# Seven block products for both FFN output products of a diffusion layer, with weight sums made by accumulating DMAs

## The chip, the cores and the metric

One core of a Trainium2 chip runs the whole layer as one program. The metric is the device time of one execution in microseconds (us). TensorE (PE in the profile) multiplies, VectorE (DVE) and ScalarE (ACT) work on tiles in SBUF and PSUM, GpSimd (POOL) adds tiles and can issue DMAs, and SyncE (SP) issues DMAs. Each engine carries out its own instructions in order, and waits at an instruction until what it reads and overwrites is ready.

## The reference

The layer works on 1024 latent tokens and 256 context tokens of width 1024. It has a half-step FFN, a token mixer and a second half-step FFN, and ends with an RMSNorm. The part that is changed:

```python
def swiglu(h, w_in, w_out):
    a, b = jnp.split(h @ w_in, 2, axis=-1)
    return (jax.nn.silu(a) * b) @ w_out
...
x = x + 0.5 * ml[2] * swiglu(modulate(rms_norm(x, norm1_g[layer]), ml[0], ml[1]),
                              ffn1_w_in[layer], ffn1_w_out[layer])
...
x = x + 0.5 * ml[8] * swiglu(modulate(rms_norm(x, norm3_g[layer]), ml[6], ml[7]),
                              ffn2_w_in[layer], ffn2_w_out[layer])
return rms_norm(x, final_g)
```

The hidden width D_FF is 2816, which is 22 row blocks of 128. Everything is float32.

## The kernel before

Activations lie transposed in SBUF: 128 channels on the partitions, tokens along the row. The latent tokens are two chunks of 512, C0 and C1. A float32 product is made of three products in the faster float32r format: each operand is split into a high part (a cast, on ScalarE) and a low part (the source less the high part, a subtraction on VectorE; `split`, L186), and high·high, high·low and low·high are summed in PSUM. So one 128x128 block of weights against 512 tokens costs three matmuls.

The FFN's in-product (class `Winograd`, L463 to 740) already uses a scheme with seven products instead of eight. It makes the hidden rows j = 0 to 21, both chunks of one j at a time. Its right operands, the tiles r of eight kinds (28 tiles for one FFN), stay in SBUF meanwhile.

The **out-product of FFN1** (L1029 to 1066) is a plain product. The hidden rows were stored in DRAM (`hd`, by `spill`, L963) and are loaded again, 256 KB each, and split; for each chunk and each group of three output blocks d the columns of w_out are loaded (`load_w`, L202), split and multiplied: 8 d x 22 j x 2 chunks x 3 = 1056 matmuls of 512 columns. At the end of each group the result is scaled by a gate and added to x (a SCALAR_TENSOR_TENSOR on VectorE). Between them, in C0, the generator `steps` is run four steps at a time; it makes the adaLN modulation from w_mod (`later_mod`, L261: loads of 256 KB called rawm, and accumulations macc on VectorE). In C1 the generator `norms2` (`norm0`, L499) is run, which prepares chunk C0 for the mixer: sum of squares, rstd, scaling, and the split into r1 and r2.

The **out-product of FFN2** (`ffn`, L742 to 786) is woven into its in-product: after every two hidden rows j come their 96 matmuls into all eight blocks d and both chunks, and each result is added to x at once, 16 adds for each of 11 pairs. The hidden rows never leave SBUF. In the last pair C1 is done as two halves of 256 columns, so that the final norm of C0 (`final`, L1488) runs beside them.

Between both FFNs lies the mixer: the mix stage (L1070 to 1112) makes gates and convolution inputs, attention follows.

The tile pools set what can run ahead: the A pool has 38 slots of 4 KB a partition (x, r, hidden rows and much else; `A_BUFS`), raw weights have 3 buffers, split weights wl and wh 4 each, short-lived tiles (`ttile`) 11; PSUM has five banks under the tag s (names ps), two under t (pt) and one under o (po). A scheduler orders the instructions of each engine by data and buffers; SyncE's queue holds nearly all DMAs. Because every instruction is recorded in one helper, the profile gives L88 for all; the tile names tell them apart.

Of the kernel before, what the change touches and what calls it, by code (L numbers as in the profile page):

```python
# [49 lines left out]
def tile_dit_layer(  # L50
# [79 lines left out]
    def matmul(out, w, x, start, stop, pinned=False):  # L130
        inst = pe.matmul(out, w, x, start=start, stop=stop)
        if pinned:
            tc.keep_in_program_order(inst)
# [329 lines left out]
    class Winograd:  # L463
# [6 lines left out]
        def __init__(self, xs, gain, mod, m, pairs, plain=False, ahead=3, side_from=None):  # L470
# [9 lines left out]
            self.n_ahead, self.side, self.started, self.n_left = ahead, None, [], 0  # L480
            self.source, self.ready = self.lefts(pairs, side_from), []
# [32 lines left out]
        def square(self, d):  # L514

            if d == 0:
                self.acc = [ttile("sq_acc")]
            sq = self.acc[0] if d == 0 else ttile("sq")
            act.activation(out=sq, in_=self.xs(d, C1), func=AF.Square)
            if d == KD - 1:  # L520
                self.acc.append(sq)
            elif d:
                dve.tensor_add(out=self.acc[0], in0=self.acc[0], in1=sq)

# [217 lines left out]
        def ffn(self, w_o, gate, last_chunks, after):  # L742
            def hidden(a, b, j, ch):

                if j % 2 == 0:
                    t = atile("hid", (P, 2, 512), F32R)
                    g = t[:, 0], t[:, 1]
                else:
                    g = ttile("gh", dt=F32R), ttile("gl", dt=F32R)
                act.activation(out=a, in_=a, func=AF.Silu)  # L750
                dve.tensor_mul(out=a, in0=a, in1=b)
                split(a, *g)
                hid[j, ch] = g

            for pr in range(NH // 2):
                hid = {}
                js = (2 * pr, 2 * pr + 1)
                if pr == 0:
                    self.start(self.norm1())
                for j in js:  # L760
                    u, c = self.next_first()
                    v, b = self.second(u)
                    hidden(c, b, j, C0)
                    hidden(*self.third(u, v), j, C1)
                ws = out_pieces(w_o, js)
                if pr < NH // 2 - 1:
                    self.prefetch(3)
                for ch in (C0, C1) if pr < NH // 2 - 1 else last_chunks:
                    s, o, n = ch
                    full = (C0, C1)[o // 512]  # L770
# [340 lines left out]
    for k in range(4):  # L1111
        mix.part_second(k)
# [462 lines left out]
```

## Time and profile before

| quantity | value |
|---|---|
| time, median of 3 runs | 2805.99 us (2802.83 to 2806.69) |
| profiled execution, time | 2801.0 us |
| profiled execution, span of its trace | 2799.2 us |
| granted TensorE clock, mean | 0.987 |
| matmuls | 13741 |
| DMA, mean | 108 GB/s |

The span is divided into busy time by engine; the chain is the sequence of instructions and waits that ended last. A window row gives, for one stretch of time, the busy time and number of instructions of each engine, then the granted clock of TensorE, the share of the DMA engines and their GB/s. A row of groups reads: engine, operation, output <- inputs (without the numbers of buffers), shapes and count, then busy time in us and mean ns of one, then the idle time just before and what ended it. A timeline row gives the start and length in us, and in brackets the idle time before it.

### The profile page before, as it was taken

To read this page: it belongs to the slowest core of one execution; us is meant where nothing else is said; L and a number is where in the kernel's file an instruction comes from. 1 tells how busy PE (TensorE), PEld (TensorE's weight loads), DVE (VectorE), ACT (ScalarE), POOL (GpSimd) and SP (SyncE) were. 2 spreads that over 40 slices of the span, in tenths; PEclk is the share of its full clock that TensorE was granted. 3 is DMA by queue.
4 is the path that set the end of the run, shared out by engine and by line. 5 is a ranking of instruction groups with operands and counts; after the bars stand their busy time and mean duration, and the time that the engine had idled before them with its cause. 6 is when DMAs were issued, how large, how long until landed. Compare 5 with 4: busy or idle time off the path is not lost.

```text
span 2799.2 us, 36980 instructions
## 1 busy us (share of the span) xinstructions
PE 2716.4 (97%) x13741; PEld 2280.3 (81%) x13741; DVE 1956.4 (70%) x3269; ACT 1105.1 (39%) x2177; POOL 502.6 (18%) x383
## 2 busy tenths in 40 slices
PE   7898999999999989999999999999998999999998
PEld 4687988888888867888999888877886788888887
DVE  5887688877854398676478676675458766666667
ACT  4524333333433243333244665674235222332225
POOL 2240122121000043323023111000002221212110
PEclk8899999999999999999999999999999999999999
DMA  8264434445974333322312321002433311111111
GB/s 305 95 204 156 143 107 128 131 145 162 314 237 126 103 123 106 98 90 77 119 33 84 95 80 46 27 31 80 158 91 103 101 46 46 61 61 53 46 53 68
DMA packets 355229, 302.96 MB, mean 108 GB/s; under 512 B 25558, under 2 KB 284776, under 8 KB 355048
## 3 DMA queue, kind: packets, MB, share of 16 engines
q1 hardware_dynamic: 355048, 300.59, 33.3%
q8 instruction: 108, 1.77, 0.3%
q14 instruction: 73, 0.60, 0.1%
HBM read 251.73 MB, written 48.76 MB: 107 GB/s over the span
## 4 chain that ended last, share of the span: by engine, by line
PE 54%; DVE 4%; ACT 1%; issue 1%; DMA 1%; DVEq 0%; ACTq 0%
PE ps L88 48%; PE po L88 3%; PE pt L88 3%; DVE wl L88 1%; DVE xb L88 0%; DMA raw<-in_ffn_w_out_dram 0%; DVE r L88 0%; DVE u L88 0%; DVE nt L88 0%; DVE ol L88 0%; DVE wo L88 0%; ACT pts L88 0%; DVE pts L88 0%; ACT pl L88 0%; DVE uc L88 0%
## 5 line engine op out<-in xcount | busy, mean ns | idle before, releaser
L88 PE MATMUL ps<-r,wl 128*128 128x512 f32 x5280 | 1237.7, 393 | 31.8 <-ACT wl L88 9.6
L88 PEld LDWEIGHTS ps<-r,wl 128*128 128x128 f32 x5280 | 992.2, 189 | 250.2 <-ACT wl L88 11.9
L88 POOL TENSOR_TENSOR s<-raw 128x512 f32<-128x512 f32 x64 | 100.7, 1573 | 1100.0 <-DVE r L88 377.5
L88 ACT CAST wl<-s 128x512 fp32r<-128x512 f32 x256 | 158.3, 620 | 318.9 <-PE ps L88 266.3
L88 ACT CAST wl<-raw 128x512 fp32r<-128x512 f32 x230 | 142.5, 621 | 251.9 <-PE ps L88 170.6
L88 DVE TENSOR_TENSOR wl<-raw,wl 128x512 fp32r<-128x512 f32 x228 | 163.0, 715 | 96.9 <-ACT wl L88 95.9
L88 POOL TENSOR_TENSOR s<-raw,s 128x512 f32<-128x512 f32 x64 | 102.5, 1601 | 686.1 <-DVE wl L88 682.5
L88 DVE TENSOR_TENSOR wl<-s,wl 128x512 fp32r<-128x512 f32 x256 | 215.8, 844 | 9.7 <-ACT wl L88 7.7
L88 PE MATMUL ps<-hid,wh 128*128 128x512 f32 x704 | 217.2, 390 | 0.7 <-ACT wh L88 0.7
L88 DVE SCALAR_TENSOR_TENSOR x<-ps,gate_l,x 128x512 f32<-128x512 f32 (+1 forms) x200 | 140.7, 726 | 76.7 <-PE ps L88 76.5
L88 ACT CAST wh<-raw 128x1024 fp32r<-128x1024 f32 (+2 forms) x92 | 89.4, 976 | 198.0 <-PE ps L88 167.8
L88 PEld LDWEIGHTS ps<-hid,wh 128*128 128x128 f32 x704 | 131.7, 188 | 29.5 <-ACT wh L88 1.6
L88 DVE SCALAR_TENSOR_TENSOR macc<-rawm,silu_c,macc 128x512 f32<-128x512 f32 x168 | 140.8, 856 | 15.2 <-DMA rawm<-in_w_mod_dram 14.1
L88 PE MATMUL ps<-hid,wo 128*128 128x512 f32 (+1 forms) x552 | 147.8, 381 | 2.3 <-DVE x L88 2.3
L88 DVE TENSOR_TENSOR u<-u,ps 128x512 f32<-128x512 f32 x168 | 114.2, 680 | 45.4 <-PE ps L88 45.0
L88 DVE TENSOR_TENSOR wl<-raw,wh 128x1024 fp32r<-128x1024 f32 (+1 forms) x84 | 98.4, 1172 | 65.5 <-ACT wh L88 64.0
L88 PE MATMUL ps<-wh,r 128*128 128x256 f32 x768 | 141.6, 285 | 0.0
L88 DVE TENSOR_TENSOR pts<-pt,pts 128x512 fp32r<-128x512 f32 x160 | 108.6, 686 | 43.1 <-ACT pts L88 41.9
L88 PE MATMUL ps<-hid,wl 128*128 128x512 f32 x352 | 136.5, 389 | 0.0
L88 PE MATMUL ps<-gh,wo 128*128 128x512 f32 (+1 forms) x368 | 135.0, 380 | 0.0
L88 DVE TENSOR_REDUCE m<-ps 128x1 f32<-128x512 f32 (+1 forms) x192 | 110.9, 595 | 26.6 <-PE ps L88 25.6
L88 ACT CAST pts<-pt 128x512 fp32r<-128x512 f32 x160 | 93.1, 593 | 86.2 <-PE pt L88 84.6
(254 smaller groups left out, 4784.4 us busy)
## 6 DMA issues: line engine op xcount, KB each, us to landing
raw<-in_ffn_w_in_dram SPq DMA_DIRECT2D x114, 512.0 KB, 3.7
raw<-in_ffn_w_out_dram SPq DMA_DIRECT2D x76, 512.0 KB, 4.3
rawm<-in_w_mod_dram SPq DMA_DIRECT2D x128, 256.0 KB, 3.9
raw<-in_w_in_dram SPq DMA_DIRECT2D x57, 512.0 KB, 3.6
hid<-hd SPq DMA_DIRECT2D x44, 256.0 KB, 6.1
rawm<-in_w_mod_dram SPq DMA_DIRECT2D x16, 512.0 KB, 7.3
xd<-x SPq DMA_DIRECT2D x32, 256.0 KB, 2.5
x<-xd SPq DMA_DIRECT2D x32, 256.0 KB, 5.9
```

Of the source, the lines that this page charges most:

```text
L88: inst = getattr(self.engine, name)(*args, **kw)
```

## The change

Both out-products become `row_products`. The hidden matrix H (22 row blocks x 1024 tokens) and the weights W (22 row blocks x 1024 outputs) are cut in halves both ways: b11 and b12 are H's rows 0 to 10 in C0 and C1, b21 and b22 its rows 11 to 21; W00, W01 are W's rows 0 to 10 for output blocks 0 to 3 and 4 to 7, W10, W11 its rows 11 to 21. Each of the seven products has 11 rows x 4 output blocks x 3 = 132 matmuls, in this order:

| product | left | right | added to (first block, chunk) |
|---|---|---|---|
| 1 | W00 | b11 | (0, C0) |
| 2 | W10 | b21 | (0, C0) |
| 4 | W11 | b21 − b22 + b12 − b11 | (4, C0) |
| 5 | W01 + W11 | b12 − b11 | (0, C1), (4, C1) |
| 6 | W00 − W01 − W11 | b12 − b11 − b22 | (0, C1), with product 1 |
| 7 | W00 − W01 | b22 − b12 | (4, C0), (4, C1), with 1 and 6 |
| 3 | W00 + W10 − W01 − W11 | b22 | (0, C1) |

Products 1, 6 and 7 accumulate one after another in the same four PSUM banks (pt, pt, po, ps), which are read between them. The sums of H are made in place by VectorE. The sums of W are made by DMAs that GpSimd issues and that add a block of w_out in DRAM to a tile in SBUF (`plus`: 24 for each FFN, 20 of 512 KB and 4 of 256 KB); the negations are ScalarE's (`minus`). Rows go in groups of two (tiles of 128x1024). A whole FFN has 36 adds into x.

FFN2 now makes all 22 hidden rows first, stores them in `hd` and loads them again, and its product 3 comes in two halves of 256 columns. In FFN1 the squares for the second norm come in the order 4 to 7, 0 to 3; 63 steps of `steps` move into the mix loop, eleven for each i above 1. `final` takes its blocks in the order 4 to 7, 0 to 3, makes yf on VectorE, and runs in smaller steps within product 3.

The order of instructions at three places. First, VectorE at the end of FFN1's out-product before (x1 is the latent stream, pt the norm's row factors, r1 the mixer's right operand, ps the result that is added):

```order
L88 TENSOR_TENSOR x1_1183_6842<-x1_1183_6842,pt_1368_8006 128x512
L88 TENSOR_TENSOR wl_1394_8142<-raw_1392_8140,wh_1393_8141 128x1024
L88 TENSOR_TENSOR r1_1369_8013<-x1_1180_6836,r1_1369_8013 128x512
L88 SCALAR_TENSOR_TENSOR x1_1331_7763<-ps_1335_7775,gate1_l_6724,x1_1331_7763 128x512
L88 TENSOR_TENSOR r1_1370_8018<-x1_1181_6838,r1_1370_8018 128x512
L88 TENSOR_TENSOR r1_1371_8023<-x1_1182_6840,r1_1371_8023 128x512
L88 TENSOR_TENSOR wl_1397_8172<-raw_1395_8170,wh_1396_8171 128x1024
```

and now, in two pieces, at the end of product 3; first the add of its first bank and the norm's multiplications (eight in all):

```order
L88 SCALAR_TENSOR_TENSOR x1_1184_6806<-ps_1382_8101,gate1_l_6724,x1_1184_6806 128x512
L88 TENSOR_TENSOR x1_1180_6794<-x1_1180_6794,pt_1410_8243 128x512
L88 TENSOR_TENSOR x1_1181_6796<-x1_1181_6796,pt_1410_8243 128x512
L88 TENSOR_TENSOR x1_1182_6798<-x1_1182_6798,pt_1410_8243 128x512
L88 TENSOR_TENSOR x1_1183_6800<-x1_1183_6800,pt_1410_8243 128x512
L88 TENSOR_TENSOR x1_1180_6794<-x1_1180_6794,pt_1410_8243 128x512
```

Right behind the eighth multiplication, the other three adds, two weight splits of the mixer and r1's low parts:

```order
L88 SCALAR_TENSOR_TENSOR x1_1185_6808<-ps_1383_8102,gate1_l_6724,x1_1185_6808 128x512
L88 SCALAR_TENSOR_TENSOR x1_1186_6810<-ps_1384_8103,gate1_l_6724,x1_1186_6810 128x512
L88 SCALAR_TENSOR_TENSOR x1_1187_6812<-ps_1385_8104,gate1_l_6724,x1_1187_6812 128x512
L88 TENSOR_TENSOR sq_acc_1378_8087<-sq_acc_1378_8087,sq_1431_8377 128x512
L88 TENSOR_TENSOR wl_1439_8401<-raw_1438_8399,wl_1439_8401 128x512
L88 TENSOR_TENSOR wl_1440_8404<-raw_1438_8399,wl_1440_8404 128x512
L88 TENSOR_TENSOR r1_1411_8250<-x1_1180_6794,r1_1411_8250 128x512
L88 TENSOR_TENSOR r1_1412_8255<-x1_1181_6796,r1_1412_8255 128x512
```

The norm's multiplications and r1's low parts stood between weight splits and adds in the middle of the out-product's last part; now they stand behind the add of product 3's first bank, and r1 behind all four adds.

Second, VectorE in FFN1's out-product before, where the first adds of C0 fall (macc is the modulation, sq the squares):

```order
L88 TENSOR_TENSOR wl_1296_7535<-raw_1294_7533,wh_1295_7534 128x1024
L88 TENSOR_TENSOR accl_1276_7409<-macc0_1257_7293,acch_1275_7408 128x512
L88 SCALAR_TENSOR_TENSOR x1_1180_6836<-ps_1241_7186,gate1_l_6724,x1_1180_6836 128x512
L88 TENSOR_TENSOR wl_1299_7565<-raw_1297_7563,wh_1298_7564 128x1024
L88 SCALAR_TENSOR_TENSOR x1_1181_6838<-ps_1242_7187,gate1_l_6724,x1_1181_6838 128x512
L88 TENSOR_TENSOR sq_acc_1344_7844<-sq_acc_1344_7844,sq_1346_7848 128x512
L88 TENSOR_TENSOR sq_acc2_1345_7845<-sq_acc2_1345_7845,sq_1347_7851 128x512
```

and now in product 1, around group 3 (hid 1159 is b12's group 0 and hid 1161 b22's; 1166 and 1167 are b11's and b12's group 2):

```order
L88 TENSOR_TENSOR wh_1206_6899<-hid_1166_6756,wh_1205_6898 128x1024
L88 TENSOR_TENSOR hid_1166_6756<-hid_1167_6757,hid_1166_6756 128x1024
L88 TENSOR_TENSOR hid_1159_6749<-hid_1161_6751,hid_1159_6749 128x1024
L88 SCALAR_TENSOR_TENSOR macc0_1133_6623<-rawm_1135_6627,silu_c_93,macc0_1133_6623 128x512
L88 TENSOR_TENSOR wl_1209_6930<-raw_1207_6927,wl_1208_6929 128x1024
L88 SCALAR_TENSOR_TENSOR macc0_1133_6623<-rawm_1136_6630,silu_c_93,macc0_1133_6623 128x512
L88 TENSOR_TENSOR wh_1211_6934<-hid_1170_6760,wh_1210_6933 128x1024
L88 SCALAR_TENSOR_TENSOR macc0_1133_6623<-rawm_1137_6633,silu_c_93,macc0_1133_6623 128x512
L88 TENSOR_TENSOR hid_1170_6760<-hid_1171_6761,hid_1170_6760 128x1024
```

The weight split remains; a split of a hidden tile and a subtraction of two hidden tiles come with each group, and product 6's subtraction of b22's group 0 stands already here. Third, GpSimd around FFN1's out-product before (s1 to s3 are sums of in-product weights; the first four rows belong to the FFN's in-product, the last to the mixer):

```order
L88 TENSOR_TENSOR s1_1093_6329<-raw_1092_6327 128x512
L88 TENSOR_TENSOR s2_1094_6330<-s1_1093_6329,raw_1091_6325 128x512
L88 TENSOR_TENSOR s3_1095_6331<-raw_1091_6325,raw_1092_6327 128x512
L88 TENSOR_TENSOR s2_1094_6330<-raw_1091_6325,s2_1094_6330 128x512
L88 TENSOR_TENSOR s1_1500_8824<-raw_1499_8822 128x512
```

and now (ws is the tile in which the sums for products 5, 6 and 3 grow, raw the one for product 7):

```order
L88 DMA ws_1283_7365<-in_ffn1_w_out_dram 128x2x512
L88 DMA ws_1289_7402<-in_ffn1_w_out_dram 128x2x512
L88 DMA ws_1295_7439<-in_ffn1_w_out_dram 128x512
L88 DMA raw_1348_7864<-in_ffn1_w_out_dram 128x2x512
L88 DMA raw_1353_7906<-in_ffn1_w_out_dram 128x2x512
L88 DMA raw_1358_7942<-in_ffn1_w_out_dram 128x2x512
L88 DMA ws_1265_7254<-in_ffn1_w_out_dram 128x2x512
L88 DMA ws_1271_7291<-in_ffn1_w_out_dram 128x2x512
```

Where GpSimd had nothing, it now issues 24 accumulating DMAs, and the first three of product 7 stand ahead of those for product 6.

The diff, cut to its core:

```diff
+    def row_products(w, rows, add, after=lambda i, k: None, halves=False):
+        R, groups = P * rows.n, rows.groups
...
+        def plus(t, *kmlr):
+            pool.dma_start(out=t, in_=block(*kmlr), accum_op=ALU.add)
+        def minus(t):
+            act.activation(out=t, in_=t, func=AF.Copy, scale=-1.0)
...
+            b11, b12, b21, b22 = (rows.t[k, v, c] for v in range(2) for c in range(2))
+            if i == 1:
+                left = part_of_w(k, m, 0, 0)
+            elif i == 2:
+                left = part_of_w(k, m, 1, 0)
+            elif i == 4:
+                left = part_of_w(k, m, 1, 1)
+            elif i == 7:
+                left = part_of_w(k, m, 0, 1)
+                minus(left)
+                plus(left, k, m, 0, 0)
+            else:
+                left = sums[k]
+            right = {1: b11, 2: b21, 4: b21, 5: b11, 6: b11, 7: b12, 3: b22}[i]
+            l, r = parts(left, m, tags[0]), parts(right, m, tags[1])
+            if i == 1:
+                dve.tensor_sub(out=b11, in0=b12, in1=b11)
+            elif i == 2:
+                dve.tensor_sub(out=b21, in0=b21, in1=b22)
+                dve.tensor_add(out=b21, in0=b21, in1=b11)
+            elif i == 4:
+                sums[k] = atile("ws", (P, 2, 512))[:, :m]
+                load(sums[k], block(k, m, 0, 1))
+                plus(sums[k], k, m, 1, 1)
+            elif i == 5:
+                minus(sums[k])
+                plus(sums[k], k, m, 0, 0)
+                dve.tensor_sub(out=b11, in0=b11, in1=b22)
+            elif i == 6:
+                plus(sums[k], k, m, 1, 0)
+                dve.tensor_sub(out=b12, in0=b22, in1=b12)
+            return l, r
+        def steps_of(i, ps, k, m, l, r, a=0, n=512):
+            on = i in (6, 7)
+            for e in range(m):
+                for d in range(4):
+                    wh, wl = (t[:, e, d * P : (d + 1) * P] for t in l)
+                    xh, xl = (t[:, e, a : a + n] for t in r)
+                    matmul(ps[d], wh, xh, start=not on and k + e == 0, stop=False, on=on)
+                    matmul(ps[d], wh, xl, start=False, stop=False, on=on)
+                    matmul(ps[d], wl, xh, start=False, stop=k + e == rows.n - 1, on=on)
...
+        chain = [ps_t(), ps_t(), ps_o(), ps_s()]
+        for i in (1, 2, 4, 5, 6, 7) + (() if halves else (3,)):
+            ps = chain if i in (1, 6, 7) else [ps_s() for _ in range(4)]
+            for k, m in groups:
+                steps_of(i, ps, k, m, *operands(i, k, m))
+                after(i, k)
+            for o, ch in to[i]:
+                for d in range(4):
+                    add(o + d, ch, ps[d])
+            after(i, rows.n)
...
+        if (i, k) == (7, 0):
+            gain2.update(norm_gain("gain2", 3, "g2"))
+            mix.gain = gain2["l"]
+        if k == NH // 2:
+            if i == 2:
+                done(range(4), C0)
+            elif i == 7:
+                done(range(4, KD), C0)
+                done(range(4, KD), C1)
+            elif i == 3:
+                done(range(4), C1)
+        if i == 3 and k in (0, 2, 4, 6):
+            run(norms2, 1)
+    row_products(ffn1_w_out[0], hs, add1, after1)
...
+        if i > 1:
+            run(steps, 11)
...
+    fast.start(fast.norm1())
+    for j in range(NH):
+        u, c = fast.next_first()
+        v, b = fast.second(u)
+        spill(c, b, j, C0)
+        spill(*fast.third(u, v), j, C1)
+    hs = Rows(NH // 2, "hid")
+    hs.fetch(hd)
...
+    def after3(i, k):
+        if i == 9 and k < NH // 2:
+            run(finals[0], 3)
+        if (i, k) == (8, NH // 2):
+            run(finals[0], 2)
+        if i == 9 and k >= 4 and k < NH // 2:
+            run(finals[1], 4)
+    row_products(ffn2_w_out[0], hs, add3, after3, halves=True)
```

190 lines of the change are left out of this document (93 added, 97 removed).

## The prediction

> **What bounds the kernel now.** I read the page's busy shares and chain first, then windows over the stretches that the change touches.
>
> ```profile
> span 2799.2 us, 36980 instructions
> PE 2716.4 (97%) x13741; PEld 2280.3 (81%) x13741; DVE 1956.4 (70%) x3269; ACT 1105.1 (39%) x2177; POOL 502.6 (18%) x383
> PE 54%; DVE 4%; ACT 1%; issue 1%; DMA 1%; DVEq 0%; ACTq 0%
> ```
>
> TensorE is busy 97% of the span, and it alone carries the chain (no other engine over 4%). So matmuls that go are time saved, unless something that feeds them becomes late. By stretch (FFN1's out-product, the first stretch of the mix, its steady part, FFN2, tail):
>
> ```profile
> core 0: us, PE busy (x) PEld busy (x) DVE busy (x) ACT busy (x) POOL busy (x), PEclk, DMA share, GB/s
> 719.00:963.00 244.00, 243.25 (x1079) 199.91 (x1078) 130.54 (x182) 83.34 (x112) 0.00 (x0) 1.00 0.62 198
> 963.00:1077.00 114.00, 103.44 (x439) 81.81 (x437) 102.17 (x162) 47.13 (x84) 43.84 (x23) 0.96 0.38 123
> 1077.00:1365.00 288.00, 287.80 (x1270) 238.38 (x1271) 200.31 (x300) 95.33 (x158) 84.06 (x57) 1.00 0.29 93
> 2176.00:2733.00 557.00, 554.71 (x2442) 457.55 (x2441) 371.93 (x531) 149.75 (x255) 104.78 (x76) 1.00 0.19 59
> 2733.00:2799.20 66.20, 56.59 (x331) 49.02 (x329) 49.02 (x113) 36.19 (x72) 1.30 (x1) 0.97 0.16 64
> ```
>
> Both out-products lie in stretches where PE waits for almost nothing (0.8 us of 244, 2.3 of 557) and VectorE has 113 and 185 us free. The mix's start is different: PE idles 10.6 us of 114 there, and VectorE is 90% busy.
>
> **PE: what goes.** The price of one matmul is the distance between starts.
>
> ```profile
> 2359.80 38.24 PE L88 MATMUL ps<-r,wl 128*128 128x512 f32 x168
> 2397.88 2.20 PE L88 MATMUL ps<-hid,wo 128*128 128x512 f32 x9
> ...
> 2768.17 0.28 PE L88 MATMUL ps<-gh,wo 128*128 128x256 f32 x1
> 2768.29 0.28 PE L88 MATMUL ps<-gl,wo 128*128 128x256 f32 x1
> ...
> L88 PE MATMUL ps<-hid,wh 128*128 128x512 f32 x704 | 217.2, 390 | 0.7 <-ACT wh L88 0.7
> L88 PE MATMUL ps<-hid,wl 128*128 128x512 f32 x352 | 136.5, 389 | 0.0
> ```
>
> 168 matmuls take 2397.88 − 2359.80 = 38.08 us: 0.2267 us for 512 columns; 0.12 us for 256. FFN1's out-product is 704 + 352 = 1056 matmuls now, 239.4 us; seven products of 11 rows x 4 column blocks x 3 are 924, 209.5 us (29.9 each): **−29.9 us**. FFN2's is 1008 of 512 and 96 of 256 columns (code: ten pairs of 96, the last pair 48 + 96), 240.0 us; six products of 132 and one in two halves of 132 each make 792 and 264, 211.2 us: **−28.8 us**. Together **−58.7 us**.
>
> **VectorE and ScalarE in a product.** Each product splits a left and a right operand, 11 rows each.
>
> ```profile
> L88 DVE TENSOR_TENSOR wl<-raw,wh 128x1024 fp32r<-128x1024 f32 x32 | 39.1, 1223 | 23.0 <-ACT wh L88 22.6
> L88 DVE SCALAR_TENSOR_TENSOR macc<-rawm,silu_c,macc 128x512 f32<-128x512 f32 x28 | 21.0, 749 | 4.5 <-DMA rawm<-in_w_mod_dram 4.0
> L88 DVE TENSOR_TENSOR hid<-hid 128x512 fp32r<-128x512 f32 x23 | 15.1, 693 | 11.4 <-ACT hid L88 11.4
> L88 DVE SCALAR_TENSOR_TENSOR x<-ps,gate_l,x 128x512 f32<-128x512 f32 x15 | 11.2, 747 | 12.1 <-PE ps L88 12.1
> L88 ACT CAST wh<-raw 128x1024 fp32r<-128x1024 f32 x30 | 31.5, 1050 | 61.3 <-PE ps L88 45.9 <-DMA raw<-in_ffn_w_out_dram 15.5
> ```
>
> One operand costs VectorE 5 x 1.22 + 0.69 = 6.8 us a product, one pass of subtraction as much. Products 1, 5 and 6 need 3 passes, 20.4 us, product 2 needs 4, 27.2, the others 13.6; adds into x at 0.75 bring 3 to 6. Seven products: (14 splits + 5 passes) x 6.8 + 36 adds x 0.75 = 156 us beside 209.5 on PE. It fits as a sum. ScalarE's 14 x 6 x 1.05 = 88 us and the negations do too. FFN1's first two products are the tight place: 47.6 us of passes, four adds (3), eight accumulations of the modulation (6), eight context updates of 0.5 (4), leftovers of the context product, and product 6's subtraction, which the order puts there, all beside 59.8 us of PE. That subtraction also makes VectorE wait for block 22, the last to be loaded: behind it stand the splits of groups 4 and 5, and PE has 5.4 us of work a group in hand. I take **+4 us** (0 to 10). FFN2's in-product loses the out-product that was woven in.
>
> ```profile
> L88 DVE SCALAR_TENSOR_TENSOR x<-ps,gate_l,x 128x512 f32<-128x512 f32 x160 | 115.4, 747 | 61.5 <-PE ps L88 61.3
> 400.00:500.00 100.00, 100.00 (x565) 86.96 (x564) 82.60 (x130) 33.60 (x60) 21.20 (x13) 1.00 0.38 116
> ```
>
> VectorE loses these 160 adds there, 115 of its 372 us, when PE loses some 218 of 555 (ten pairs x 96 x 0.2267): 257 us beside 337, 76%. FFN1's in-product (second row) keeps PE at 100 of 100 us with VectorE at 83%: 0.
>
> PSUM: product 4 needs product 2's four banks back, product 3 those of product 5 and product 7 the chain's after product 6's adds. The last group is one row, 12 matmuls or 2.7 us, and its bank d is done 0.68 (3 − d) us before the end; four adds at 0.75 finish about 1 us after it, and PE comes back to bank d after 0.68 d. **+2 us** for both FFNs (0 to 6).
>
> **The accumulating DMAs**, 24 in each FFN, are an operation that this trace doesn't have.
>
> ```profile
> q1 hardware_dynamic: 355048, 300.59, 33.3%
> q8 instruction: 108, 1.77, 0.3%
> q14 instruction: 73, 0.60, 0.1%
> raw<-in_ffn_w_out_dram SPq DMA_DIRECT2D x76, 512.0 KB, 4.3
> hid<-hd SPq DMA_DIRECT2D x44, 256.0 KB, 6.1
> DMA  9999999996956974598992232207722342462304
> GB/s 331 375 364 390 305 346 332 306 269 171 298 169 205 305 227 123 158 341 266 352 313 78 64 89 86 86 6 228 219 65 75 117 129 83 159 192 87 90 0 129
> ```
>
> Every data packet went through one hardware queue; GpSimd's isn't there. The nearest row is a plain load of 512 KB, 4.3 us to landing; the largest transfer rate, 390 GB/s, would give 1.3, and a sum that reads its destination, adds and writes it may cost several times 4.3. I bound it by 1.3 and 13 (three plain landings) and take 6. What counts is how late it may come. The sums for product 5 are issued in product 4, those for 6 in 5, those for 3 in 6: one product (29.9 us) ahead or more, six to a product. If they run one after another at T, sum k of product 5 is there at about (k + 1) T + 3 after product 5's start and wanted at 29.9 + 5.4 k; for the last that is 6 T + 3 against 57, so up to T = 9 nothing waits. Product 7's first three sums go ahead of this; its last three need a raw buffer, a load of 4.3, a negation of 1.05 and T, and have some 14 us: T up to about 9 again. At 6 the cost is **0** (at the upper end 6 x 13 + 3 − 57 = 24 late at products 5 and 6 of each FFN, 96 us if nothing overlaps; that is the slower case below). The Trainium skill, "DMA: Bandwidth & Descriptors", section "Anatomy of one DMA — SWDGE (gpsimd) path", fits a DMA issued by GpSimd with 2.0 us + bytes / 436e3: an estimate of 3.2 us for 512 KB, with which the sum stays as it is; no row here can show it, and it speaks of plain transfers.
>
> **Mix start.** Now TensorE goes from the out-product into the mix without a pause, because norm and split of r1 were finished inside the out-product:
>
> ```profile
> 962.96 0.39 PE L88 MATMUL ps<-hid,wl 128*128 128x512 f32 x1
> 963.19 2.88 PE L88 MATMUL ps<-r,wl 128*128 128x512 f32 x12
> ...
> 996.70 8.15 PE L88 MATMUL ps<-r,wl 128*128 128x512 f32 x26 [3.84 <-ACT wl L88]
> 996.70:1000.00 3.30, 3.30 (x8) 2.57 (x9) 3.30 (x7) 1.50 (x3) 0.73 (x1) 0.53 0.39 159
> ...
> 997.32 0.67 DVE L88 TENSOR_TENSOR nt<-h,h 128x512 f32<-128x512 f32 x1
> 997.92 0.67 DVE L88 TENSOR_TENSOR r<-nt,r 128x512 fp32r<-128x512 f32 x1
> ```
>
> After the change VectorE's queue holds, behind product 3's first add (which waits for PE's last row): eight multiplications by the norm, three adds, a sum, two weight splits, then r1. That add can start 2 us before PE ends. At 0.60 us from start to start (the last two rows) and 0.75 an add, 8 x 0.60 + 4 x 0.75 + 3 x 0.60 + 0.6 = 10.2 us: r1's low part comes 8 us after PE's last matmul, and PE waits for it at its second mix matmul. After an idle of 3.84 us the clock was granted at 0.53 for 3.3 us, so 1.5 us more. Some 2 us come back, because idle time that follows there now has the same cause. **+8 us** (3 to 14).
>
> **Reload before FFN2's products.** 22 tiles, 11.5 MB, come from DRAM; 36 of the 38 slots are held by r and x, and four come free with each of the last row block's products, 12 matmuls or 2.7 us apart, from some 16 us before its end. Block 22 comes behind 9.3 MB of other blocks and weights, 28 us at the 331 GB/s above: 12 us into product 1, or 14 with its own landing. VectorE's queue has its first subtraction behind group 3's split, about there. **+4 us** (0 to 12).
>
> **The rest.** 63 modulation steps move into the mix loop: about 28 accumulations x 0.75 = 21 us of VectorE where it has 88 of 288 free, and 28 loads where DMA is at 0.29: **+2** (0 to 6). Tail: four adds of 256 columns instead of eight after the last product, new order of squares; the last matmul of the FFN starts at 2785.71 and the span ends 13.5 us later in any case:
>
> ```profile
> 2785.71 0.28 PE L88 MATMUL ps<-gh,wo 128*128 128x256 f32 x1
> 2793.40 1.27 ACT L88 ACTIVATE ot<-ps,rs_y 128x512 f32<-128x512 f32 x2 [0.45 <-DVE rs_y L88]
> ```
>
> The chain add, square, sum, rstd, scaling, store stays: 0 (−2 to 2).
>
> **Sum.** The profiled execution took 2801.0 us (span 2799.2). 2801.0 − 58.7 + 4 + 2 + 0 + 8 + 4 + 2 = 2762.3, a gain of 38.7 (1.4%). That execution is 5 us under the median of 2805.99 and just below the fastest timed run; the median less 38.7 is 2767.3. I predict **2765**, between them.
>
> **Rivals.**
> *VectorE becomes the bound of the products.* For: product 2 needs 30 of 29.9 us, and the rows above show VectorE idling 23 us for ScalarE's cast, a dependence that recurs in every group. Against: two groups of operands can be ready ahead. With 85% of VectorE usable product 2's 30 us become 36 (+6 in each FFN), FFN1's first two products cost their upper 10 instead of 4, the mix start its upper 14 instead of 8: 2765 + 12 + 6 + 6 = 2789.
> *The accumulating DMAs set the pace* (slower). For: one queue, waits in order, read and write; against: one product of lead. Products 5 and 6 of both FFNs are late by 6 T + 3 − 57 each; 4 (6 T − 54) = 38.7 gives T = 10.6 us as the point where the gain is gone, and T = 12 adds 72: 2837. The Trainium skill's same page, section "Rules for kernel authors", says that an accumulate reads its destination and writes it later; sums on one tile then have to run one after another, as the code has it in any case; no row of this trace shows it.
> *Nothing is exposed:* r1 arrives early and nothing else waits: 2742.3 + 2 for the banks + the same 2.7 for the median = 2747.
> *The change doesn't cut matmuls as it says:* the rows of the changed program show 132 less in FFN1; excluded.
>
> **Chances.** Forecast (2752 to 2778) 0.50; VectorE bound (2778 to 2800) 0.20; nothing exposed 0.08; stalls of both kinds that about cancel the gain 0.05; accumulates pace 0.17. A measurement of this kernel tells 0.2% (5.6 us) from no change. Faster 0.78, same 0.05, slower 0.17. The range 2738 to 2812 leaves out most of the last case and a little below the third.
>
> **What will show it.** PE's instructions must fall by some 130 before the mix, and product 1 to product 3 of FFN1 take about 215 us. Right for the mix start: an idle of PE of about 8 us released by VectorE's r just after product 3, with a granted clock of about a half behind it. Wrong: PE waiting for casts of ws or raw (that the releaser is a DMA then says that the accumulates pace), or an idle of PE at product 1 of FFN2 released by hid<-hd. The forecast fails if T is above 9 us or if VectorE is over 95% busy through the products.

## The result and the profile after

The changed kernel takes 2803.14 us (median of 12 runs, 2797.40 to 2809.71), the kernel before 2805.28 us in the same comparison (12 runs, 2800.69 to 2807.82). The ratio is 0.9997, 95% interval 0.9988 to 1.0006. That is no change that can be measured: 59 us of matmul work are gone and the time is not. The forecast of 2765 is 38 us off. The wide range of 2738 to 2812 holds the result, but only as the case "stalls of both kinds that about cancel the gain", which had been given a chance of 0.05; that is luck, not a merit of the working.

First the page of the changed kernel: span, engines, the chain by engine, GpSimd's DMA queue and the hardware queue, and the loads and sums of w_out (KB each, median us from issue to landing).

```profile
span 2801.6 us, 36926 instructions
PE 2685.7 (96%) x13625; PEld 2254.8 (80%) x13625; DVE 1981.3 (71%) x3204; ACT 1151.6 (41%) x2165; POOL 565.7 (20%) x431
PE 58%; DVE 6%; issue 3%; ACT 1%; DMA 1%; POOL 0%; POOLq 0%; ACTq 0%; DVEq 0%
q1 hardware_dynamic: 333128, 317.90, 34.4%
q0 software_dynamic: 12032, 23.07, 5.2%
raw<-in_ffn_w_out_dram SPq DMA_DIRECT2D x62, 512.0 KB, 5.4
ws<-in_ffn_w_out_dram POOLq DMA_DIRECT2D x30, 512.0 KB, 6.5
raw<-in_ffn_w_out_dram POOLq DMA_DIRECT2D x10, 512.0 KB, 5.8
```

TensorE is busy 30.7 us less than before, and the span is 2.4 us longer. So TensorE now waits, and part of its busy time runs at a lower clock (0.978 on the mean, 0.987 before). The sums land in 6.5 and 5.8 us: the 6 us that the prediction took. The windows tell where the waits are: product 1, product 2 and product 6 of FFN1, the mix's start, FFN2's in-product alone, then FFN2's products in two parts.

```profile
core 0: us, PE busy (x) PEld busy (x) DVE busy (x) ACT busy (x) POOL busy (x), PEclk, DMA share, GB/s
721.68:756.00 34.32, 29.87 (x131) 23.85 (x130) 32.65 (x37) 10.71 (x13) 1.35 (x1) 1.00 1.03 388
756.00:789.00 33.00, 32.59 (x136) 26.43 (x136) 29.98 (x35) 12.41 (x14) 5.21 (x5) 0.95 0.92 250
855.00:888.00 33.00, 30.28 (x130) 24.32 (x130) 18.74 (x21) 11.63 (x13) 7.03 (x6) 1.00 0.55 84
956.17:1032.80 76.63, 60.46 (x236) 45.82 (x237) 66.81 (x114) 43.29 (x78) 21.70 (x9) 0.87 0.34 111
2166.68:2530.00 363.32, 363.32 (x1603) 300.94 (x1604) 231.38 (x318) 117.34 (x191) 115.98 (x81) 1.00 0.32 103
2538.00:2690.00 152.00, 140.11 (x591) 113.32 (x590) 104.77 (x106) 61.57 (x66) 21.33 (x18) 0.96 0.68 174
2690.00:2787.00 97.00, 93.50 (x561) 84.35 (x560) 52.61 (x95) 35.56 (x53) 6.68 (x6) 0.95 0.28 62
```

FFN2's in-product keeps TensorE busy in every microsecond. The products do not: each has 29.9 us of matmuls and takes 33.5 on the average in FFN1 (234.5 us for seven), with the clock at 0.95 to 0.96 in several stretches, and the mix's start has 16 us without a matmul.

Three marks divide the span: the first matmul of FFN1's out-product, the last transposition of the norm ahead of FFN2, and the end.

| kernel | first mark | first to second (FFN1, mix, attention) | second to the end (FFN2, tail) |
|---|---|---|---|
| before | 719.1 | 1398.1 | 682.0 |
| predicted, from the terms of the sum | 719.1 | 1383.2 | 658.2 |
| after | 721.7 | 1398.1 | 681.8 |

(The banks' 2 us are halved between the FFNs. The first mark differs by up to 5 us among runs of kernels that are alike up to there.) The missing gain is 15 us in the first part and 24 in the second.

**A boundary between two products.** VectorE and TensorE where product 5 of FFN1 ends and product 6 begins:

```profile
851.90 1.23 DVE L88 TENSOR_TENSOR wl<-ws,wl 128x1024 fp32r<-128x1024 f32 x1 [3.85 <-ACT wl L88]
853.05 2.72 DVE L88 SCALAR_TENSOR_TENSOR x<-ps,gate_l,x 128x512 f32<-128x512 f32 x4
855.68 1.22 DVE L88 TENSOR_TENSOR wh<-hid,wh 128x1024 fp32r<-128x1024 f32 x1
854.25 0.39 PE L88 MATMUL ps<-wh,wl 128*128 128x512 f32 x1
856.95 1.20 PE L88 MATMUL pt<-wh,wl 128*128 128x512 f32 x4 [2.32 <-DVE wh L88]
```

Product 5's last matmul starts at 854.25, product 6's first waits until 856.95 for the low part of its right operand. VectorE makes that part behind the left operand's and behind four adds of product 5's result. Two groups of operands fit in the tiles wl and wh, so it can begin only when the last full group has been multiplied, and from there TensorE has the one-row group left, 12 matmuls or 2.7 us, against 1.23 + 2.72 + 1.22 = 5.2 us on VectorE. In FFN1 idles of 0.8 to 2.8 us stand at every boundary but the first, 9.6 us in all: 5.9 of them end with such a split, 3.7 with an add into x that gives a PSUM bank back and stands in the same queue of VectorE.

**The queue of the accumulating DMAs.** GpSimd's issues in FFN1, from the fourth of product 5's six sums on:

```profile
779.36 1.23 POOL L88 DMA_DIRECT2D ws<-in_ffn_w_out_dram  x1 [6.33 <-issue]
787.46 2.15 POOL L88 DMA_DIRECT2D ws<-in_ffn_w_out_dram  x2 [6.88 <-issue]
808.37 1.22 POOL L88 DMA_DIRECT2D raw<-in_ffn_w_out_dram  x1 [18.77 <-ACT raw L88]
817.34 1.21 POOL L88 DMA_DIRECT2D raw<-in_ffn_w_out_dram  x1 [7.75 <-ACT raw L88]
823.91 1.22 POOL L88 DMA_DIRECT2D raw<-in_ffn_w_out_dram  x1 [5.36 <-ACT wl L88]
830.02 1.21 POOL L88 DMA_DIRECT2D ws<-in_ffn_w_out_dram  x1 [4.88 <-issue]
...
898.60 1.21 POOL L88 DMA_DIRECT2D raw<-in_ffn_w_out_dram  x1 [6.44 <-issue]
904.71 2.17 POOL L88 DMA_DIRECT2D raw<-in_ffn_w_out_dram  x2 [4.90 <-issue]
```

Product 5's sums (ws) are out by 789.6, well ahead. Then three of product 7's (raw) stand in the queue, wait 18.8 us for their load and negation, and from there one sum follows another every 6 to 7 us. Product 7's last three are issued at 898.60 and later, when product 7 has been running since 888; there TensorE waits 2.21 us (906.51), the only wait for sums that shows in FFN1. In FFN2 the sums for product 3 come late too, since the order there weaves product 3's first half into product 6 (ScalarE and TensorE):

```profile
2679.39 1.04 ACT L88 CAST kept<-ws 128x1024 fp32r<-128x1024 f32 x1 [12.04 <-DMA ws<-in_ffn_w_out_dram]
2681.43 0.79 PE L88 MATMUL ps<-kept,kept 128*128 128x256 f32 x2 [5.46 <-ACT kept L88]
```

**The mix's start.** TensorE waits for r1 twice, then for weights:

```profile
960.54 0.79 PE L88 MATMUL ps<-r,wl 128*128 128x512 f32 x1 [4.37 <-ACT r L88]
964.62 8.09 PE L88 MATMUL ps<-r,wl 128*128 128x512 f32 x26 [3.29 <-DVE r L88]
...
998.64 1.98 PE L88 MATMUL ps<-r,wl 128*128 128x512 f32 x5 [2.53 <-ACT wl L88]
```

From its first matmul (963.19 before, 956.17 the end of the products after) to a group of 58 matmuls that both kernels have (1022.22 and 1024.97), the mix's start takes 59.0 us before and 68.8 after.

### The profile page after: what moved, and what is told of

Same layout as the page of the kernel before. It is cut to its first block, busy times and chain, and to the rows that moved or that the text cites. A ratio compares the mean times of both kernels' runs of the same rounds, so it can differ in the third digit from the quotient of the medians.

```text
span 2801.6 us, 36926 instructions
## 1 busy us (share of the span) xinstructions
PE 2685.7 (96%) x13625; PEld 2254.8 (80%) x13625; DVE 1981.3 (71%) x3204; ACT 1151.6 (41%) x2165; POOL 565.7 (20%) x431
## 4 chain that ended last, share of the span: by engine, by line
PE 58%; DVE 6%; issue 3%; ACT 1%; DMA 1%; POOL 0%; POOLq 0%; ACTq 0%; DVEq 0%
PE ps L88 48%; PE pt L88 5%; PE po L88 4%; DVE wl L88 1%; DVE r L88 1%; DVE nt L88 1%; DMA raw<-in_ffn_w_out_dram 1%; DVE y L88 0%; DVE x L88 0%; POOL ws L88 0%; ACT wl L88 0%; DVE ol L88 0%; DMA ws<-in_ffn_w_out_dram 0%; DVE h L88 0%; DVE pts L88 0%
## 5 line engine op out<-in xcount | busy, mean ns | idle before, releaser
L88 ACT CAST wl<-raw 128x512 fp32r<-128x512 f32 (+1 forms) x278 | 189.2, 683 | 401.1 <-PE ps L88 297.1
L88 DVE TENSOR_TENSOR wl<-raw,wl 128x512 fp32r<-128x512 f32 (+1 forms) x276 | 220.5, 800 | 165.2 <-ACT wl L88 159.7
L88 PE MATMUL ps<-wh,wl 128*128 128x512 f32 x1122 | 277.2, 395 | 10.7 <-DVE wh L88 5.2
L88 PEld LDWEIGHTS ps<-wh,wl 128*128 128x128 f32 x1122 | 213.0, 190 | 59.4 <-DVE wh L88 7.0
L88 PE MATMUL pt<-wh,wl 128*128 128x512 f32 x396 | 110.9, 402 | 15.7 <-ACT wh L88 5.7
L88 PEld LDWEIGHTS ps<-wh,r 128*128 128x128 f32 x768 | 120.6, 192 | 0.0
L88 PE MATMUL po<-pts,vh 128*128 128x512 f32 x256 | 110.3, 437 | 1.5 <-ACT pts L88 1.5
L88 PE MATMUL ps<-wl,r 128*128 128x256 f32 x384 | 108.8, 283 | 0.0
L88 PE MATMUL ps<-kl,qs 128*128 128x512 f32 x384 | 106.0, 397 | 0.4 <-ACT pc L88 0.4
L88 PEld LDWEIGHTS pt<-wh,wl 128*128 128x128 f32 x396 | 74.7, 193 | 34.9 <-DVE wh L88 7.6
```

The costliest lines, as they stand in the source:

```text
L88: inst = getattr(self.engine, name)(*args, **kw)
```

## The experiments

Four theories stood at the beginning. A: the cover at a product's boundary is too short. B: VectorE's load (the sums of H above all) delays the operands. C: the accumulating DMAs come late. D: A and C hide one another, so that either alone gives little back. Ratios are to the kernel before, with 95% intervals.

### e1: the one-row group third instead of last

```diff
-self.groups = [(k, min(2, n - k)) for k in range(0, n, 2)]
+self.groups = [(0, 2), (2, 2), (4, 1), (5, 2), (7, 2), (9, 2)]
```

The norm's steps within product 3 are called at the groups 0, 2, 4 and 5.

> The one-row group of each product stands third instead of last (rows 0-1, 2-3, 4, 5-6, 7-8, 9-10); nothing else changes. Theory A (short cover: at each product's end PE has only a one-row group of 2.7 us in hand, while VectorE's queue has split, four adds and split of about 5.3 us before the next product can go on): the twelve boundaries lose about 2.3 us of idle and 1 of slow clock each now, a one-row group inside a product costs about 1 us each, so 15 to 25 us less than the changed kernel, about 2780 to 2788. Theory B (VectorE's load, the sums of H) and theory C (the accumulating DMAs): within 3 us of the changed kernel's 2803.

2799.19 us, 0.9984 (0.9975 to 0.9993). The idles at the boundaries are gone (0.18 us is left in FFN1), but the time is only 4 us better, not the 15 to 25 of A. In their place stand longer waits for sums, at product 7 of FFN1 and at product 3's operands in FFN2 (the casts named here as releasers stand behind a cast that waited for the DMA of the sum), and product 1 of FFN1 idles 6.4 us instead of 4.45:

```profile
902.52 1.22 PE L88 MATMUL pt<-wh,wl 128*128 128x512 f32 x2 [7.89 <-ACT wh L88]
...
2673.82 1.22 PE L88 MATMUL ps<-kept,kept 128*128 128x256 f32 x4 [7.56 <-ACT kept L88]
```

### e2: the one-row group left out of every product

```diff
-self.groups = [(k, min(2, n - k)) for k in range(0, n, 2)]
+self.groups = [(k, min(2, n - k)) for k in range(0, n - 1, 2)]
```

> Left out: the one-row group of every product in both FFNs, so ten rows of eleven are multiplied (the output lacks two hidden row blocks). This takes away 2 x 7 x 12 matmuls of 0.2267 us, 38 us of PE's work. Theory A: the boundaries get 5.4 us of cover too, 20 to 30 us beyond the 38: 2735 to 2745. Theories B and C: 38 and about a tenth of the stalls: 2757 to 2765.

2777.99 us, 0.9906 (0.9891 to 0.9920). With 38 us less work for TensorE it gains 25, less than either expectation. The two waits of e1 grow to 10.17 and 11.71 us: TensorE has less to do, but the chain of sums hardly gets shorter, since only the four small sums of each FFN go.

### e3: no accumulating DMAs

```diff
-            pool.dma_start(out=t, in_=block(*kmlr), accum_op=ALU.add)
+            return
```

> Left out: all 48 accumulating DMAs, so the weight sums lack their second to fourth blocks; loads, negations, splits and matmuls stay. Theory C: most of the lost 58 us comes back, 25 us or more below the changed kernel. Theory A: only the waits that product 7 (2.2 us in FFN1) and product 3 of FFN2 (5.5, 1.0 and 2.5 us) show go, with the slow clock behind them: 10 to 15 us, 2788 to 2793. Theory B: the same as A.

2790.97 us, 0.9952 (0.9937 to 0.9966): 12 us better than the changed kernel, within A's 10 to 15 and less than the 25 or more of C. The mix's first matmul comes 9.0 us sooner (229.8 against 238.9 after the first mark; 4.7 of it are the products, 4.4 a wait for r1 in the changed kernel), but the second mark comes no sooner: 1399.1 us after the first. The mix takes the gain back, most of it in one wait (2.53 us in the changed kernel), for a weight cast that stands on ScalarE behind the casts of the normed operands, which VectorE makes:

```profile
995.43 6.91 PE L88 MATMUL ps<-r,wl 128*128 128x512 f32 x21 [9.74 <-ACT wl L88]
```

FFN2, which has no such stage behind it, keeps its gain: 667.7 against 681.8.

### e4: no sums of H

The five in-place passes by `dve.tensor_sub` and `dve.tensor_add` in `operands` are left out.

> Left out: the five subtractions and additions of hidden tiles of each group, so the right operands are the plain blocks; all else stays. It takes 34 us of VectorE's time out of each FFN. Theory B: products 1 and 2 run at PE's pace in both FFNs (about 8 and 3.5 us back) and the boundaries too: 20 us or more. Theory A: the 8 to 11 us of products 1 and 2 only, the boundaries at products 4 to 3 stay: 2792 to 2797. Theory C: 0.

2805.87 us, 1.0007 (0.9998 to 1.0017). Nothing is gained, and the idles at the boundaries are the same. Product 1 of FFN1 idles 1.43 us instead of 4.45, but 1.77 us come in product 2. B falls, as far as it rests on the sums of H.

### e5: e1 and e3 together

> The one-row group stands third, and all accumulating DMAs are left out (the weight sums are wrong by that). Theory D (boundaries and accumulating DMAs hide one another: with the boundaries mended PE runs into the chain of sums, which come one every 6 to 7 us, 24 to an FFN): both together give far more than 4 + 12, about 35 us, 2765 to 2772. Theory C (only the sums matter): 2788 to 2791, as without the sums alone. Theory A (only the boundaries): 2799 less the waits of products 7 and 3, about 2785.

2770.76 us, 0.9879 (0.9864 to 0.9893): 32 us better than the changed kernel, twice the sum of e1's 4 and e3's 12. D is right. The products now run with almost no idle (FFN1's products 2 to 3, then all of FFN2's):

```profile
756.00:946.00 190.00, 187.37 (x824) 153.03 (x823) 133.03 (x159) 87.65 (x103) 0.00 (x0) 1.00 0.25 87
2528.00:2755.00 227.00, 225.41 (x1145) 192.41 (x1144) 156.13 (x195) 97.42 (x119) 0.00 (x0) 0.98 0.25 91
```

By the marks it takes 1387.6 and 659.4 us, where the prediction's terms gave 1383.2 and 658.2. With the two causes out, the rest of the sum holds within 6 us. (This kernel leaves the sums out, so it shows what they cost with all that hangs on them; e9 below makes them in another way.)

### e6, e7, e8: GpSimd makes the sums; x is loaded later; both

In e6 the group stands as in e1, and each sum is a plain load and a `pool.tensor_add` or `tensor_sub`. In e7 FFN1's loads of x are issued behind the first group of products 1, 2 and 4. e8 has both and sums the final norm's squares on VectorE.

```diff
-                plus(sums[k], k, m, 1, 1)
+                pool.tensor_add(out=sums[k], in0=sums[k], in1=left)
```

> The one-row group stands third, and the sums of weights are made by GpSimd from plainly loaded tiles (one addition or subtraction of 128x1024 a group, about 3.1 us by twice the 1.57 of 128x512) in place of the negation and the accumulating DMA. Theory D: the sums come at least twice as fast, so nearly what leaving them out gives: 2768 to 2778. Rival (GpSimd's additions slow VectorE, or the extra plain loads crowd the DMA queues): no better than 2795.

> The one-row group stands third, and in FFN1 the 16 loads of x (4 MB) are issued after the first group of products 1, 2 and 4 instead of all ahead of product 1. In the run with the group moved PE waited 6.0 us in product 1 for a weight tile whose load stood behind these loads in SyncE's queue. Theory D: these 6 us and about 3 of slow clock go from product 1 of FFN1, and come back in part at the chain of sums: 2793 to 2797. If the loads are not the cause, 2799.

> One-row group third, sums by GpSimd, late loads of x, and in the final norm the eight squares of a chunk are summed on VectorE before PE's one-column products (16 of them instead of 80). Theory D: 8 us below the kernel with the first two edits for the loads, and 7 of PE's time and some 5 of slow clock in the tail: about 2755 to 2765. If each gain is taken back by the next limit again: above 2780.

e6: 2805.85 us, 0.9998 (0.9989 to 1.0008). e7: 2803.03, 0.9993 (0.9984 to 1.0002). e8: 2802.85, 0.9991 (0.9981 to 1.0000). None gains on e1 or on the changed kernel. In e6 GpSimd's sum and VectorE's pass over H hold one another up; VectorE first, then GpSimd:

```profile
846.20 3.32 DVE L88 TENSOR_TENSOR hid<-hid,hid 128x1024 f32<-128x1024 f32 x1
845.10 3.33 POOL L88 TENSOR_TENSOR ws<-raw,ws 128x1024 f32<-128x1024 f32 x1 [2.30 <-DVE wl L88]
```

The pass takes 3.32 us where it takes 1.22 alone: it starts after GpSimd's sum and ends 1.09 us behind it, as if it had waited for the whole of it. GpSimd's sum takes 3.33 us here and 2.40 at 802.40, where VectorE idles. In e7 most of the stall moves from product 1 (now 2.25 us) to product 2 (5.3 us); all that is loaded stays the same, and the DMA engines are full:

```profile
730.00:770.00 40.00, 35.99 (x148) 28.30 (x146) 37.32 (x42) 13.87 (x15) 4.71 (x4) 0.96 1.06 366
```

### e9, e10: VectorE makes the sums, all or all but product 5's

As e6, with `dve` for `pool`; in e10 product 5's six sums of an FFN stay accumulating DMAs.

> The one-row group stands third, and VectorE makes the weight sums from plainly loaded tiles, 1.22 us for 128x1024 in place of a negation and an accumulating DMA. Theory D (serial sums by DMA, one every 6 to 7 us, hide the gain): the chain of sums is gone, VectorE gets 27 us more work in an FFN; product 5 has 32 us of VectorE's work in 30, so 5 to 15 us above the run without any sums (2771): 2775 to 2786. Rival (VectorE is the next limit everywhere): above 2795.

> As the run before, but the six sums of product 5 of each FFN (negation and block 00) stay accumulating DMAs, the other eighteen are VectorE's. Six DMAs of 6 to 7 us have a product of lead and nothing queued ahead of them. Theory D: like the run before or up to 5 us less, since product 5 has 26 us of VectorE's work now: 2772 to 2782. If any accumulating DMA costs, however much lead it has: 2785 or more.

e9: 2782.05 us, 0.9920 (0.9905 to 0.9935). e10: 2784.66, 0.9931 (0.9915 to 0.9946). Both compute the whole layer and are faster than both kernels; e10 misses its 2772 to 2782 by 3 us and can't be told from e9. In FFN2, e9's TensorE is busy 223.73 of 230 us although VectorE has 24 sums more:

```profile
2536.00:2766.00 230.00, 223.73 (x1121) 189.68 (x1120) 177.86 (x214) 85.04 (x103) 0.00 (x0) 0.99 0.35 126
```

So the disputed sums cost little on the engine that has room, 77% busy there.

### e11: e10 with the norm one group earlier

The first step of `norms2` runs behind product 7, the other three at groups 0, 2 and 4 of product 3; the final squares are summed on VectorE.

> The run before, and the four steps of the mixer's first norm start behind product 7 instead of behind the first group of product 3, each one group (5.4 us) earlier; the eight squares of the final norm are summed on VectorE. If the mix's start waits for r1 because of the norm's chain: its idle of 13 us in the runs with the group moved falls by 5 to 8, and 2 to 3 of slow clock; the tail gives 5 more: 10 to 14 us less than the run before, 2760 to 2770. If VectorE's queue behind product 3's adds holds r1 in any case: 5 less.

2782.53 us, 0.9922 (0.9907 to 0.9936): no difference from e10 that can be told (by the marks 4.5 us less in the second part, where the tail's squares are, and 3.5 more in the first). The idles at the mix's start are the same, 2.27, 4.92 and 5.80 us, since VectorE's order did not change where it counts:

```profile
943.59 0.75 DVE L88 SCALAR_TENSOR_TENSOR x<-ps,gate_l,x 128x512 f32<-128x512 f32 x1 [1.68 <-PE ps L88]
944.47 4.87 DVE L88 TENSOR_TENSOR x<-x,pt 128x512 f32<-128x512 f32 x8
```

The multiplications by the norm still stand behind product 3's first add, which waits for TensorE's last row.

### e12: e1 with each accumulating DMA of 512 KB as two of 256 KB

```diff
-            pool.dma_start(out=t, in_=block(*kmlr), accum_op=ALU.add)
+            k, m, lower, right = kmlr
+            for e in range(m):
+                pool.dma_start(out=t[:, e : e + 1], in_=block(k + e, 1, lower, right), accum_op=ALU.add)
```

> The one-row group stands third, and each accumulating DMA of 512 KB is made as two of 256 KB one after another: the same bytes, 80 more DMAs. If the time of an accumulating DMA goes by its bytes: 2799, as with the group moved alone. If each costs several us on its own and they wait for one another: two take 8 us or more instead of 6 to 7, and products 4 to 7 grow by 40 us or more in each FFN: above 2860.

2790.06 us, 0.9942 (0.9925 to 0.9958), 9 us better than e1: neither expectation. The halves are issued 2 to 3 us apart, not 3 to 3.5:

```profile
765.21 0.89 POOL L88 DMA_DIRECT2D ws<-in_ffn_w_out_dram  x1 [4.95 <-issue]
767.24 0.88 POOL L88 DMA_DIRECT2D ws<-in_ffn_w_out_dram  x1 [1.15 <-PE ps L88]
769.21 0.86 POOL L88 DMA_DIRECT2D ws<-in_ffn_w_out_dram  x1 [1.09 <-issue]
```

The execution that was profiled took 2801.8 us, 12 more than the median, so its marks say nothing on the gain. Yet the waits for sums are shorter in it: none at product 3's operands in FFN2 (7.56 in e1), and at product 7 of FFN1 1.12 us (7.89 in e1):

```profile
907.96 0.73 PE L88 MATMUL pt<-wh,wl 128*128 128x512 f32 x2 [1.12 <-ACT wh L88]
```

Product 6's sums take 30.5 us from their first issue to product 3's first, and 35.4 in e1. So faster sums are worth something; why two halves are faster than one whole was not settled.

### e13, e14: which of the sums are late

Both have e1's groups. In e13 only product 7's sums are VectorE's, and 18 accumulating DMAs remain in an FFN; in e14 only product 7's six remain.

> The one-row group stands third, and product 7's sums (W00 less W01) are made by VectorE from plain loads; the other 18 sums of an FFN, each issued a product ahead, stay accumulating DMAs. If what is late is product 7's sums, which have no lead and hold the queue while they wait for a load and a negation, this gives what the version with only product 5's six accumulating DMAs gave, about 2785. If it is the rate at which sums follow one another in one queue (18 at 6 to 7 us, 110 to 125 us, wanted within three products of 30), product 3's sums stay late and it is at 2793 to 2799. I hold the first for likelier, at about 2787.

> The one-row group stands third, and only product 7's six sums of an FFN stay accumulating DMAs; VectorE makes the other 18 from plain loads. If the queue's rate is at fault, six in an empty queue cost nothing: about 2783. If it is the missing lead (a raw buffer, a load of 5, a negation of 1, a sum of 6 us, with two of three raw buffers taken by other loads), PE still waits some 5 to 8 us at product 7 of each FFN and the time is 2790 to 2797. By the theory of the missing lead it is slower than the run before this one; by that of the rate it is faster.

e13: 2800.28 us, 0.9983 (0.9974 to 0.9992). e14: 2789.10, 0.9943 (0.9930 to 0.9955). I held product 7's sums to be the fault, and that fell: taking them out alone brings nothing over e1's 2799.19. In FFN1 the wait at product 7 falls from 7.89 to 3.56 us, and VectorE's sum waits there for a plain load that comes late; in FFN2 the wait for product 3's sums stays (7.53 us). The rate of the others weighs more, as these issues of e13 show (FFN1, products 6 and 3):

```profile
826.94 1.22 POOL L88 DMA_DIRECT2D ws<-in_ffn_w_out_dram  x1 [33.00 <-ACT ws L88]
...
862.97 1.22 POOL L88 DMA_DIRECT2D ws<-in_ffn_w_out_dram  x1 [5.51 <-DVE wl L88]
...
892.03 1.20 POOL L88 DMA_DIRECT2D ws<-in_ffn_w_out_dram  x1 [6.97 <-DVE x L88]
```

Six sums take 862.97 − 826.94 = 36.0 us, a product has 29.9 us of matmuls, and the first of product 6's cannot start before product 5 has used the tile (33 us of waiting). e14 is not free either, 7 us over e9 with intervals that touch; in FFN1 TensorE waits 3.45 us at its product 7 in three pieces, in FFN2 not at all. So the missing lead has a part in FFN1, smaller than expected. The marks come from the one profiled execution of each (e14 2785.43 us, 4 under its median; e9 2785.48, 3 above its own):

| kernel | first to second mark | second to the end |
|---|---|---|
| e1 (24 accumulating DMAs in an FFN) | 1399.3 | 678.0 |
| e13 (18, product 7's out) | 1400.6 | 677.1 |
| e14 (6, product 7's) | 1399.0 | 664.1 |
| e10 (6, product 5's) | 1392.9 | 667.8 |
| e9 (none) | 1394.9 | 666.2 |
| e5 (none, and nothing in their place) | 1387.6 | 659.4 |

In FFN2 the eighteen for products 5, 6 and 3 cost 11 us (e13 against e9), product 5's six alone 2 (e10) and product 7's nothing (e14). In FFN1 the differences to e9 are between −2 and +6, within the scatter of single profiles. The twelve for products 6 and 3 were not tried alone.

## Why the prediction was wrong, point by point

- **The matmuls that go: −58.7, right.** The work is gone: 132 matmuls fewer in FFN1, 48 fewer in FFN2, and e5 comes to the predicted time within 6 us by the marks. (The whole count falls by 116 only, because of 64 new small ones in the tail, below.)
- **The accumulating DMAs: 0, wrong. This is the step that failed.** T was right (5.8 to 6.5 us for a predicted 6). The Trainium skill, "DMA: Bandwidth & Descriptors", section "Anatomy of one DMA — SWDGE (gpsimd) path", fits a DMA issued by GpSimd with 2.0 us + bytes / 436e3; the estimate of 3.2 us by it is half of what the trace shows, and the section has no time for an accumulating DMA. The rule made from T, "up to T = 9 nothing waits", was wrong. It set one product's sums against their own deadline, 6 T + 3 against 57, and forgot that three sets follow one another in one queue. Sums of product 6 can start only as product 5 uses its tiles up, and so on; six of them take 36.0 us in e13, and 31.2 and 37.4 in the changed kernel, of every 29.9, so a product loses up to 7 us of its lead. By this estimate T would have to be below about 29.9 / 5.5 = 5.4 us (five whole sums and a half one), not 9. Product 7's first three sums were said to go ahead, but were given no time: they hold the queue for 18.8 us. And FFN2's product 3 is woven into product 6, so its sums have no product of lead. The price, with the boundaries mended, is 30 us by the marks: e1 to e5, 11.7 in the first part and 18.6 in the second. Of what was to show a failure, T did not pass 9 us (on the median) and VectorE reached 95% in product 1 only; the cast of ws that waits for a DMA did come (12.04 us, in FFN2).
- **The boundaries: +2 as a matter of PSUM banks, mis-sized.** The price, with the sums out, is some 20 us by the marks: e3 to e5, 11.5 and 8.3 (of the 11.5, 8.4 in the products, the rest in the mix's start). The banks have a part in it (3.7 of 9.6 us of idle in FFN1); the operands, which the sum did not count there, have the larger. The statement that TensorE has 5.4 us of work a group in hand is true of full groups; the last group has 2.7. A wait can also cost more than its own length: behind the 2.96 us of idle in product 1 the clock was granted at 0.68 for 3.5 us, and behind 2.21 us in product 7 at 0.60. Behind the idles of 1.35, 2.17 and 2.32 us at the boundaries it was 1.00, so the length alone does not tell.
- **The two together.** They do not add up, and neither do the two prices: whichever wait goes, the other fills its place, 4 + 12 us alone and 32 together. The rival of the accumulating DMAs named the right wait at a T that was too high and at the wrong place (products 5 and 6 in both FFNs; the waits came at product 7 of FFN1 and product 3 of FFN2, and product 5's six alone cost nothing that can be told, e10).
- **Products 1 and 2 of FFN1: +4, about right in size, right in part in cause.** TensorE idles 4.45 us of product 1 and 0.41 of product 2:

```profile
750.76 1.20 PE L88 MATMUL pt<-wh,wl 128*128 128x512 f32 x4 [1.48 <-ACT wl L88]
755.84 0.73 PE L88 MATMUL pt<-wh,wl 128*128 128x512 f32 x2 [2.96 <-DVE wl L88]
```

The second wait is for VectorE's split, which stands behind two subtractions of hidden tiles and a split; VectorE does not idle there, as it would if it waited for block 22. Without the subtractions (e4) product 1 idles 1.43 us, but 1.77 us come in product 2 and nothing is gained. The DMA engines are full all this while (1.03 in product 1's window; 1.01 in e5, which has no accumulating DMAs and idles 6.4 us), and e7 shows that later loads of x only move the wait. Which of the two sets the pace was not separated.

- **VectorE as the bound: rightly set behind.** It is 95% busy in product 1 (32.65 of 34.32) and 57% in product 6; e9 gives it 48 more sums and gains.
- **The mix's start: +8, right.** It is +9.8, by the chain that was described: adds, eight multiplications, then r1. The clock behind the second wait was 0.50 for 3.4 us, the half that was forecast. What was missed is the wait for the weight cast some 40 us later: 2.53 us in the changed kernel, 5.8 in e1 and e5, 9.74 in e3. The mix's start takes 70.4 us in e1 and e5 and about 74 in e3, so it can take back what the products ahead of it gain, all of it in e3, little in e5.
- **FFN2's reload: +4, and it is 1 at most.** TensorE idles 1.00 us, between products 1 and 2 (2570), with the DMA engines full until then. The in-product alone at TensorE's pace: right (363.32 of 363.32 us).
- **The mix loop: +2, and it is −0.1.** The 63 modulation steps are hidden. **Tail: 0, and it is +1.2.** Beside it, the final norm's squares come as several tiles instead of one sum, so 64 more one-column matmuls stand among the last products, a term that the sum did not have; 32 of them take 3.63 us, as much as 16 with 512 columns:

```profile
2769.50 3.63 PE L88 MATMUL pt<-ones,sq 128*128 128x1 f32 x32
```

What stays open: why e9 is 7 us behind e5 in each part (in FFN1's products 2 to 3, 5.2 us of idle are released by VectorE, in e5 0.2; the rest was not taken apart), and what sets the time of one accumulating DMA (e12).

## What to carry to other kernels

When a queue feeds several stages, compare its time for one stage with the time of that stage, not with a deadline: a lead of one stage is used up at the difference, stage by stage. Look at the smallest group at a boundary, since it and not the usual one is the cover there. When two waits lie in the same loop, take both away at once before either is called harmless; and ask what stage comes next, because a stage that is bound by another engine can take back what the one ahead of it gains.

## What the runs showed of the hardware

- An accumulating DMA of 512 KB lands in 5.8 to 6.5 us, and the next is issued 6 to 7 us after it; two of 256 KB go out 2 to 3 us apart. Between 800 and 900 us of the changed kernel, 7.34 MB of them took 46.9% of the 16 DMA engines, and 3.23 MB of plain transfers 9.5%: 6.4% for each MB against 2.9%.
- A VectorE subtraction with two inputs in SBUF takes 3.32 us instead of 1.22 beside a GpSimd sum of the same size, and the sum 3.33 instead of 2.40 (e6).
- The clock behind an idle of 2.21 us was granted at 0.60 for 3.5 us in one place, and behind idles of 2.17 and 2.32 us at 1.00 in others (changed kernel, FFN1).
